# A two-layer encoder trunk on one core: another order of seven-product pairs in the FFN down projections, activation parts made three pairs ahead, and four row loads on another queue

## The chip, the cores and the metric

The kernel runs on one core of a Trainium2 chip. The metric is the device time of one execution in microseconds; lower is better. Several executions are timed, and the median is the number that counts. One further execution is profiled; its trace is what the views below are read from.

## The reference, cut to what matters

The input is 256 frames of 2048 values in float32. Two layers follow each other; each has a token mixer and a gated MLP with a causal convolution of width 3, and each of the four sub-layers ends in a layer norm of the scaled residual plus the sub-layer's output.

```python
def conv_ffn(x, w_up, conv_w, conv_b, w_down):
    h = x @ w_up                                   # 2048 -> 2 * 5504
    h = causal_depthwise_conv(h, conv_w) + conv_b  # width 3
    a, g = jnp.split(h, 2, axis=-1)
    return (jax.nn.silu(g) * a) @ w_down           # 5504 -> 2048

def reference(x, ...):
    for i in range(2):
        m = gmlp_mixer(x, ...) if i % 2 == 0 else mla_mixer(x, ...)
        x = layer_norm(ALPHA * x + m, ln_mix_g[i], ln_mix_b[i])
        f = conv_ffn(x, ...)
        x = layer_norm(ALPHA * x + f, ln_ffn_g[i], ln_ffn_b[i])
    return x
```

Layer 0 mixes by a spatial gating MLP (`gmlp_mixer`), layer 1 by latent attention (`mla_mixer`), whose first product makes a query latent and a key/value latent, each normalised before it is used.

## The kernel before, in words

All products keep float32 accuracy by splitting each operand into a high part (a cast to the fast float32 form) and a low part (the remainder). A product of two blocks is three matmuls: high by high, low by high, high by low. Weights come as chunks of 1 MB. The class `Feed` loads a chunk into a "raw" slot through SP's queue (`_load`, L93 and L98), makes the high part on ScalarE (wh, L127) and the low part on VectorE (wl, L130), both in "big" slots, and hands them to TensorE.

A down projection (`down`) multiplies 256 frames of activations by a weight of 5504 x 2048 (in the gMLP: 6144 x 2048). It runs in two halves of 1024 output columns; each half walks over the pairs of 128-row blocks of the weight in the order that `PLAN` writes out, the second half backwards. The frames form two blocks of 128, so that one pair and half a row of outputs is a 2 x 2 by 2 x 2 block product. There are three kinds of pair:

- "e", wide: eight products of 512 columns, 24 matmuls (`Banks.eight`).
- "s", seven: the Winograd form of Strassen's product with seven products, 21 matmuls (`Banks.seven`). VectorE first forms sums of the weight blocks (ts, L137), and those are split as well (th and tl beside wh and wl), so that five big tiles are needed, of which ts is free again once tl is made.
- "p", parked: the same seven products, but the four parts of the weights were made during the up projection before (`Feed.park`), stored to DRAM by POOL's queue, and are fetched again (`Feed.fetch`, L191) into "side" slots shortly before use. This takes neither ScalarE nor VectorE in the down projection.

The last pair, 21, is half a pair. With the plan of before a half has ten or nine pairs of kinds "s" and "p", 19 in both halves.

The activations have parts as well, made by `Acts.make`: high and low for a wide pair (two wide pairs share one slot, the room), and for a seven or parked pair also the sums (`turn`, L290 to L293) and their parts (L476, L477). In the trace dn04wx are the wide parts of pair 4 in layer 0, dn119sx the seven parts of pair 19 in layer 1, and wo4wx those of pair 4 in the gMLP's output projection. At each step `down` makes the parts of the pair at hand and of the pairs ahead, then calls `feed.next`, which splits the weights two pairs ahead and loads two more, and then issues the products. While the down projection runs, act0 to act5 hold the activations (four of them in big slots, two in side slots).

```python
SLOTS = {"big": 14, "raw": 3, "side": 6}
LEAD = 5
KEEP = {"wide": 4, "seven": 6, "parked": 6}
```

The order of work is written as a program; a scheduler at build time lets an instruction pass earlier ones of its engine when these would wait, and gives a tile a slot when one is free in that order. On each engine and each queue the resulting order is fixed: a DMA that waits for a slot holds up all that its queue issues later.

The residual comes back from DRAM in two halves. `ln.fetch` (L609, SP's queue) asks for a big slot when eight pairs of a half are left. After a half's last seven or parked pair, `rest` and `fold` (L443 to L447, L648) add up the shared sums, and `piece` (L654, L657) adds the accumulators.

A layer norm leaves its result without scale and shift; the residual needs these later. `Norm.restore` (L636 to L643) loads a piece of the two rows, spread to all partitions, into two tiles "lnp" of the tag "t2", and multiplies and adds on VectorE. It is called for norm 0 and norm 2 in the up projections and for norm 1 (`idx` 1) in the latent attention's kv product (mkv), four pieces of two rows each. After that product the latents are normalised (hqk, L937), and the key's rotary part is made (kr, L983).

Of the kernel before, what the change touches and what calls it, by code (L numbers as in the profile page):

```python
# [15 lines left out]
P = 128  # L16
# [7 lines left out]
NF_FF = DFF // P  # L24
# [33 lines left out]

PLAN = {NF_GM: ("0e 1e 2s 3e 4e 5s 6e 7e 8s 9e 10e 11s 12e 13e 14s 15e 16e 17s 18e 19e 20s 21e 22e 23e",
                "23e 22e 21e 20s 19e 18e 17s 16e 15e 14s 13e 12e 11s 10e 9e 8s 7e 6e 5s 4e 3e 2e 1e 0e"),  # L60
        NF_FF: ("0e 1p 2e 3s 4e 5p 6e 7s 8e 9p 10e 11s 12e 13p 14e 15s 16e 17p 18e 19s 20e 21e",
                "21e 20e 19s 18p 17e 16s 15e 14p 13s 12e 11e 10p 9s 8e 7e 6p 5s 4e 3e 2e 1e 0e")}
KINDS = {"e": "wide", "s": "seven", "p": "parked"}
LEAD = 5
KEEP = {"wide": 4, "seven": 6, "parked": 6}
# [2 lines left out]
def plan(n_k):  # L68

    return [[(int(t[:-1]), KINDS[t[-1]]) for t in line.split()] for line in PLAN[n_k]]  # L70
# [143 lines left out]
def trunk(ctx: ExitStack, tc: tile.TileContext, x, xT, gm_in, gm_wout, ffn_up, ffn_dn,  # L214
          ml_q, ml_kv, ml_b, ml_out, consts, w_sT, b_s, ropes, ln_rows, out):
    nc = tc.nc
# [10 lines left out]
    def slot(shape, name, dt=F32, tag="big"):  # L227
        return big.tile(shape, dt, tag=tag, name=name, bufs=SLOTS[tag])
# [76 lines left out]
    for j in range(4):  # L305
        t = slot([P, 4, S], f"xraw{j}", tag="side")
# [57 lines left out]
    def prod_b(acc, parts, hi, lo, pieces, first, last):  # L364

        xh, xl = parts
        for f, (o, w) in enumerate(pieces):
            mm(acc[f][:, :w], xh, hi[:, o : o + w], first, False)
            mm(acc[f][:, :w], xl, hi[:, o : o + w], False, False)
            mm(acc[f][:, :w], xh, lo[:, o : o + w], False, last)  # L370
# [114 lines left out]
    def down(n_k, src, tag, ln, acts, skew=SKEW):  # L485

        ln.begin()
        seq = plan(n_k)
        line = seq[0] + seq[1]
        late, at = [], 0  # L490
        fetched = max([i for i, t in enumerate(line) if t[1] == "parked"], default=len(line))
        for hf, units in enumerate(seq):
            n = len(units)
            last = [u for u, kind in units if kind != "wide"][-1]
            acc = Banks(f"{tag}{hf}", OWN + DIRECT if hf else DIRECT + OWN)
            for i, (u, kind) in enumerate(units):
                left = n - 1 - i if hf == 1 else n
                for n2, v2 in enumerate(line[at : at + 2]):
                    acts.make(*v2, "side" if at + n2 > fetched or at + n2 >= len(seq[0]) and v2[1] == "parked" else "big")
                if i == n - 8:  # L500
                    ln.fetch(hf)
                got = feed.next(splits=2 if left > 5 or left == 0 else 3, loads=2 if left > 2 or left == 0 else 1)
                if left == 6:
                    ln.prep()
                a, sums = acts.got[u]
                if left < skew:
                    late.append((a, *got))
                elif kind == "wide":
                    acc.eight(a, *got)
                else:  # L510
                    acc.seven(a, sums, *got, 512 if kind == "parked" else 0)
                    if u == last:
                        for j, t in enumerate(acc.rest()):
                            ln.fold(j // 2, 2 * hf + j % 2, t)
                at += 1
                for v2 in [v2 for v2 in acts.got if not any(v2 == w2 and n2 < KEEP[kind2]
                                                            for n2, (w2, kind2) in enumerate(line[at:]))]:
                    acts.got.pop(v2)
            if hf == 0:
                for j, m in enumerate(DIRECT):  # L520
                    ln.piece(j // 2, j % 2, acc.acc[m])

        def end(b, f):
            for i, (a, hi, lo) in enumerate(late):
                for j in range(len(a[b])):
                    prod_b([acc.acc[DIRECT[2 * b + f - 2]]], a[b][j], hi, lo, [(j * 1024 + (f - 2) * 512, 512)],
                           False, i == len(late) - 1 and j == len(a[b]) - 1)

        return [[None, None] + [acc.acc[DIRECT[2 * b + f]] for f in range(2)] for b in range(2)], end
# [60 lines left out]
    class Norm:  # L590
# [42 lines left out]
        def restore(self, f):  # L633

            row = []
            for j in range(2):  # L636
                t = tp.tile([P, 512], F32, tag="t2", name=f"lnp{self.idx}_{f}{j}", bufs=T2)
                src = ln_rows[2 * self.idx + j : 2 * self.idx + j + 1, f * 512 : (f + 1) * 512]
                nc.sync.dma_start(t, src.to_broadcast([P, 512]))
                row.append(t)  # L640
            for b in range(2):
                nc.vector.tensor_tensor(self.r(b, f), self.r(b, f), row[0], ALU.mult)
                nc.vector.tensor_tensor(self.r(b, f), self.r(b, f), row[1], ALU.add)  # L643
# [184 lines left out]

    ln = Norm(0, {})
    acc, end = down(NF_GM, pT, "wo", ln, acts)  # L830


# [12 lines left out]
    def ffn(layer, ln, acc, end, last):  # L845
# [28 lines left out]
        for gi in range(1, 22):  # L874
# [20 lines left out]
            if gi == 20:  # L895
                acts.make(*plan(NF_FF)[0][2])
        ln = Norm(2 * layer + 1, {}, old.put_away, last)
        return (ln, *down(NF_FF, act, f"dn{layer}", ln, acts, 4 if last else SKEW))

    ln, acc, end = ffn(0, ln, acc, end, False)  # L900
# [75 lines left out]
    for b in range(2):  # L976
# [3 lines left out]
        t = tp.tile([P, 4, ROPE], F32, tag="t1", name=f"kr2_{b}", bufs=T1)  # L980
# [291 lines left out]
```

## Time and profile before

| | us |
|---|---|
| median of 3 timed executions | 2493.83 |
| lowest and highest | 2492.6, 2495.56 |
| the profiled execution | 2495.52 |
| its span, first to last instruction | 2493.7 |

| stage (names in the trace) | from | to |
|---|---|---|
| gMLP products, output projection (v, u, wo) | 4.8 | 802.0 |
| layer 0: up projection (up) | 802.2 | 1284.9 |
| layer 0: down projection (dn0) | 1284.8 | 1511.5 |
| latent attention (mq to mo) | 1511.7 | 1775.3 |
| layer 1: up projection (up) | 1775.5 | 2258.2 |
| layer 1: down projection (dn1) | 2258.0 | 2483.1 |

The engines: PE is TensorE, DVE is VectorE, ACT is ScalarE, POOL is GpSimd, SP is SyncE. A row of waits names the instruction that waited, then what it waited for, then the total in us, the number of times and the longest. An engine's queue for DMAs has a "q" at its name (SPq). "issue" in a chain of waits is time in which the engine waited for nothing that the profile shows. A row of a group gives the count, then busy us and the mean ns of one instruction, then the idle time before them and what ended it. The ends of matmuls are modelled, so that a busy PE is not a PE at its peak; the number of matmuls in a window says more.

### The profile page before, as it was taken

The page shows a single profiled execution, that of the slowest core. Times are in us where ns is not written, and L with a number is a line of the kernel's source. Part 1 is how long each engine was busy: PE and PEld are TensorE (multiplying, and loading weights), DVE is VectorE, ACT ScalarE, POOL GpSimd, SP SyncE. Part 2 cuts the span into 40 slices and gives each one's busy share as a digit, 9 for nine tenths or more (in the row PEclk, how much of TensorE's full clock was granted, in tenths as well). Part 3 has the DMA queues.
Part 4 walks back from the last instruction along what each step waited for, and adds up shares of the span by engine and source line. Part 5 has one row for each costly group of instructions (what it writes and reads, how often), then busy time and mean ns, then how long its engine had stood idle before and what let it go on. Part 6 is the DMA issues. An engine that isn't in the chain of part 4 may idle for free. (4 is left out here: it accounts for less than half of the span.)

```text
span 2493.7 us, 33578 instructions
## 1 busy us (share of the span) xinstructions
PE 2471.9 (99%) x12989; PEld 2121.7 (85%) x12989; DVE 2009.0 (81%) x2822; ACT 1430.9 (57%) x1983; POOL 94.6 (4%) x183
## 2 busy tenths in 40 slices
PE   9999999999999999999999999999999999999998
PEld 7888888888888888888888788988888888888786
DVE  7999866679898788788687987856598878768797
ACT  6676544456555656566554556655566656555453
POOL 0000000000000000000001000000001000000010
PEclk9999999999999999999999999999999999999999
DMA  7556554556665689799568884544489798848885
GB/s 279 202 206 225 194 177 170 182 174 214 216 199 194 235 339 348 293 345 367 194 216 315 294 325 169 191 152 152 172 295 345 294 347 330 309 163 294 333 304 206
DMA packets 111809, 620.87 MB, mean 249 GB/s; under 512 B 10528, under 2 KB 11296, under 8 KB 63392
## 3 DMA queue, kind: packets, MB, share of 16 engines
q1 hardware_dynamic: 85440, 463.51, 52.0%
q0 software_dynamic: 26208, 155.20, 16.2%
q8 instruction: 102, 1.67, 0.2%
q14 instruction: 59, 0.48, 0.1%
HBM read 546.32 MB, written 72.35 MB: 248 GB/s over the span
## 5 line engine op out<-in xcount | busy, mean ns | idle before, releaser
L130 DVE TENSOR_TENSOR wl<-raw,wh 128x1024 fp32r<-128x1024 f32 (+4 forms) x691 | 965.1, 1418 | 221.9 <-ACT wh L127 132.7
L127 ACT CAST wh<-raw 128x1024 fp32r<-128x1024 f32 (+4 forms) x691 | 816.4, 1209 | 408.4 <-PE u L234 84.5
L234 PE MATMUL up<-xhl,wh 128*128 128x512 f32 x2624 | 611.9, 390 | 0.9 <-ACT wh L127 0.9
L234 PEld LDWEIGHTS up<-xhl,wh 128*128 128x128 f32 x2624 | 487.3, 188 | 99.4 <-ACT wh L127 1.8
L234 PEld LDWEIGHTS up<-xhl,wl 128*128 128x128 f32 x2624 | 325.8, 192 | 6.4
L234 PE MATMUL up<-xhl,wl 128*128 128x256 f32 x2624 | 328.1, 283 | 0.0
L234 PE MATMUL u<-xhl,wh 128*128 128x512 f32 x768 | 184.7, 393 | 0.1
L127 ACT CAST th<-ts 128x1536 fp32r<-128x1536 f32 x106 | 110.6, 1052 | 122.2 <-DVE ts L137 107.0
L234 PEld LDWEIGHTS u<-xhl,wh 128*128 128x128 f32 x768 | 141.1, 188 | 31.6 <-issue 3.8
L130 DVE TENSOR_TENSOR tl<-ts,th 128x1536 fp32r<-128x1536 f32 x106 | 125.4, 1219 | 2.2 <-PE v_p L234 1.5
L234 PEld LDWEIGHTS u<-xhl,wl 128*128 128x128 f32 x768 | 95.4, 192 | 2.0
L234 PE MATMUL u<-xhl,wl 128*128 128x256 f32 x768 | 96.0, 283 | 0.0
L234 PE MATMUL mo<-wh,oT 128*128 128x512 f32 x256 | 83.1, 404 | 0.3 <-DVE oT L1109 0.3
L137 DVE TENSOR_TENSOR ts<-ts,raw 128x512 f32<-128x512 f32 x106 | 72.9, 688 | 1.6
L234 PE MATMUL v_q<-wh,xhl 128*128 128x512 f32 x224 | 69.9, 393 | 1.0 <-ACT wh L127 1.0
L137 DVE TENSOR_TENSOR ts<-raw 128x1024 f32<-128x1024 f32 x53 | 64.6, 1220 | 0.2 <-PE v_q L234 0.2
L234 PE MATMUL v_p<-wh,xhl 128*128 128x512 f32 x192 | 59.7, 390 | 0.4 <-ACT wh L127 0.4
L234 PEld LDWEIGHTS mo<-wh,oT 128*128 128x128 f32 x256 | 45.4, 189 | 7.6 <-DVE oT L1109 0.6
L234 PEld LDWEIGHTS v_q<-wh,xhl 128*128 128x128 f32 x224 | 42.3, 189 | 10.3 <-ACT wh L127 1.7
L234 PE MATMUL mo<-wl,oT 128*128 128x512 f32 x128 | 50.2, 392 | 0.0
L154 DVE TENSOR_TENSOR praw<-praw 128x512 f32<-128x512 f32 x72 | 49.4, 686 | 0.5
L686 ACT ACTIVATE lny<-lnt,lncol 128x128 f32<-128x128 f32 x96 | 36.6, 472 | 15.6 <-PE lnt L682 15.6
(1844 smaller groups left out, 4186.6 us busy)
## 6 DMA issues: line engine op xcount, KB each, us to landing
raw<-in_ffn_up_dram SPq DMA_DIRECT2D x172, 1024.0 KB, 6.7
raw<-in_gm_in_dram SPq DMA_DIRECT2D x93, 1024.0 KB, 4.8
raw<-in_ffn_dn_dram SPq DMA_DIRECT2D x66, 1024.0 KB, 7.1
raw<-in_gm_wout_dram SPq DMA_DIRECT2D x48, 1024.0 KB, 5.2
praw<-in_ffn_dn_dram POOLq DMA_DIRECT2D x18, 1024.0 KB, 14.4
keptth<-pth POOLq DMA_DIRECT2D x18, 1024.0 KB, 6.3
kepttl<-ptl POOLq DMA_DIRECT2D x18, 1024.0 KB, 8.9
fth<-keptth POOLq DMA_DIRECT2D x18, 1024.0 KB, 9.5
```

The costliest lines, as they stand in the source:

```text
L127: cast = self.nc.scalar.copy(hi, raw)
L130: self.nc.vector.tensor_tensor(lo, raw, hi.bitcast(F32), ALU.subtract)
L137: add = lambda o, a, b: self.nc.vector.tensor_tensor(o, a, b, ALU.add)
L154: add = lambda o, a, b: pin(nc.vector.tensor_tensor(o, a, b, ALU.add))
L234: recent[0] = nc.tensor.matmul(o, l, r, start=start, stop=stop, skip_group_check=True)
L686: nc.scalar.activation(y[:, j], t[:, j * P : (j + 1) * P], AF.Identity, bias=lncol[:, o : o + 1], scale=lncol[:, g : g + 1])
```

## The change

The plan of the FFN down projections has another order of kinds. In the first half the parked pairs are 6, 11 and 15 instead of 5, 9, 13 and 17, beside pair 1; in the second half they are 19, 15, 11 and 7 instead of 18, 14, 10 and 6. The first half has nine pairs with seven products instead of ten, the second nine as before. In `down`, which the gMLP's output projection uses too, parts are made for three pairs (the one at hand and two more) instead of two. The rows for norm 1 are loaded by POOL's queue instead of SP's.

```diff
-        NF_FF: ("0e 1p 2e 3s 4e 5p 6e 7s 8e 9p 10e 11s 12e 13p 14e 15s 16e 17p 18e 19s 20e 21e",
-                "21e 20e 19s 18p 17e 16s 15e 14p 13s 12e 11e 10p 9s 8e 7e 6p 5s 4e 3e 2e 1e 0e")}
+        NF_FF: ("0e 1p 2e 3s 4e 5e 6p 7e 8s 9e 10e 11p 12e 13s 14e 15p 16e 17s 18e 19s 20e 21e",
+                "21e 20e 19p 18e 17s 16e 15p 14e 13s 12e 11p 10s 9e 8s 7p 6e 5s 4e 3e 2e 1e 0e")}
...
-                for n2, v2 in enumerate(line[at : at + 2]):
+                for n2, v2 in enumerate(line[at : at + 3]):
...
-                nc.sync.dma_start(t, src.to_broadcast([P, 512]))
+                (nc.gpsimd if self.idx == 1 else nc.sync).dma_start(t, src.to_broadcast([P, 512]))
```

## The prediction

> **What bounds the kernel now.** I read the page first, then the waits of TensorE over the whole run, then the two stages where they fall by windows, by the order of time and by the chain of waits.
>
> ```profile
> span 2493.7 us, 33578 instructions
> PE 2471.9 (99%) x12989; PEld 2121.7 (85%) x12989; DVE 2009.0 (81%) x2822; ACT 1430.9 (57%) x1983; POOL 94.6 (4%) x183
> ```
>
> TensorE is busy for 99% of the span, so a change can gain only TensorE's few waits, and every matmul it adds is paid in full. Those of PE's waits that bear on the change (us in total, times, longest):
>
> ```profile
> PE dn_q L234 <- ACT dn019sx L476: 1.5, 1, 1.5
> ...
> PE dn_q L234 <- ACT dn119sx L476: 1.1, 1, 1.1
> ...
> PE ct L945 <- DVE hqk L937: 0.9, 1, 0.9
> PE dn_e L234 <- DVE dn017wx L480: 0.7, 1, 0.7
> PE dn_e L234 <- DVE dn117wx L480: 0.7, 1, 0.7
> PE krt L990 <- ACT kr L983: 0.6, 1, 0.6
> PE wo_q L234 <- DVE wo4wx L480: 0.6, 1, 0.6
> PE dn_q L234 <- DVE dn120wx L480: 0.6, 1, 0.6
> ```
>
> Five of these stand in the FFN down projections (dn0 and dn1 are layers 0 and 1; dn019sx is the activation parts of pair 19, "s" for seven products, "w" wide, "p" parked). What they really cost shows when matmuls are counted. Six matmuls take 1.36 us, 0.227 each (first fence below). Then windows: length, PE busy and matmuls in it, other engines in the first two rows only, the granted clock, DMA share, GB/s.
>
> ```profile
> 2259.53 1.36 PE dn_p L234 x6
> ```
> ```profile
> 1324.00:1344.00 20.00, 20.00 (x90) 16.57 (x89) 16.23 (x22) 10.27 (x12) 2.11 (x4) 1.00 0.93 336
> ...
> 1404.00:1424.00 20.00, 19.32 (x86) 15.46 (x85) 19.52 (x29) 11.37 (x12) 2.11 (x4) 1.00 0.59 203
> ```
> ```profile
> 1381.00:1391.00 10.00, 8.28 (x29) 0.83 0.88 320
> 1411.00:1416.00 5.00, 4.32 (x20) 1.00 0.69 233
> 2353.00:2361.00 8.00, 6.64 (x28) 1.00 1.04 386
> 2366.00:2371.00 5.00, 4.42 (x20) 1.00 0.92 374
> 2383.00:2388.00 5.00, 4.35 (x20) 1.00 0.65 231
> ```
>
> An undisturbed 20 us shows 90 matmuls: 20 / 0.227 is 88, and two more reach over the edges. So 10, 8 and 5 us would show 46, 37 and 24. Missing are 17, 4, 9, 4 and 4: 3.9 and 0.9 us in layer 0, 2.0, 0.9 and 0.9 us in layer 1. The two down projections lose 8.6 us. The first loss is larger than its wait, because the matmuls after it come slowly:
>
> ```profile
> 1386.12 1.05 PE L234 MATMUL dn_p<-wh,dn019sx 128*128 128x512 f32 x2
> 1386.98 0.63 PE L234 MATMUL dn_p<-wl,dn019sx 128*128 128x512 f32 x1
> ```
>
> Two matmuls start within 0.86 us, 0.43 each, at the granted clock of 0.83 in that window. The Trainium skill ("TensorE: Matmul & The Clock Gate", Why this matters for your kernels) sets the danger line at idle gaps of about 3 us; the trace disagrees, since the wait here was 1.5 us plus a second of 0.2. By that rule the slow stretch would not come from the wait and would stay, and the sum below would be smaller by 3.9 - 1.7 = 2.2 us.
>
> Why the parts of pair 19 are late is told by the chain of waits (start, length, what), layer 1:
>
> ```profile
> 2325.56 2.28 DVE tl L130 x2
> ...
> 2328.76 15.28 DMA raw<-in_ffn_dn_dram
> ...
> 2355.94 0.62 ACT dn119sx L476
> ```
> ```profile
> SPq L609 <- DVE tl L130: 30.0, 2, 15.0
> ```
>
> This is a shortage of "big" slots. The residual's fetch (L609) has to find one, and stands 15.0 us at the head of SP's queue until pair 15's tl frees its ts slot. The weights of pairs 18 and 19 queue behind it; then the fetch, weight loads and parked pair 17 travel together, and a load takes 15.28 us. ACT's cast waits for it, pair 19's sums follow, and dn119sx comes last: its room is asked for after pair 19's five weight tiles. Counted from the code, act0 to act3 hold 4 slots, the residual 1, two parts' rooms 2, pair 18's weights 2 and pair 19's 5: that is 14 of 14.
>
> **The change, part by part.**
>
> *Plan.* One parked pair less in each FFN. A wide pair makes 24 matmuls, a seven or parked one 21: 3 x 0.227 = 0.68 us more per FFN, +1.36 us, all on PE. The up projection loses per FFN one parking job (load, casts, sums, four stores), and the down projection four fetches; these lie beside TensorE's work in stages where none of the rows above stands, so I cost them at nothing. The pair that becomes wide needs one load, one cast and one subtraction. The durations (count, busy, mean ns):
>
> ```profile
> L130 DVE TENSOR_TENSOR wl<-raw,wh 128x2048 fp32r<-128x2048 f32 x15 | 34.4, 2290 | 15.1 <-ACT wh L127 10.3 <-issue 4.8
> L130 DVE TENSOR_TENSOR tl<-ts,th 128x1536 fp32r<-128x1536 f32 x8 | 14.0, 1752 | 0.0
> L130 DVE TENSOR_TENSOR wl<-raw,wh 128x1536 fp32r<-128x1536 f32 x8 | 14.0, 1751 | 0.0
> L137 DVE TENSOR_TENSOR ts<-ts,raw 128x512 f32<-128x512 f32 x17 | 11.7, 686 | 0.2
> L137 DVE TENSOR_TENSOR ts<-raw 128x1024 f32<-128x1024 f32 x9 | 11.0, 1218 | 0.0
> L130 DVE TENSOR_TENSOR tl<-ts,th 128x512 fp32r<-128x512 f32 x8 | 5.5, 684 | 0.0
> ```
> ```profile
> L127 ACT CAST wh<-raw 128x2048 fp32r<-128x2048 f32 x15 | 28.7, 1911 | 10.6 <-DMA raw<-in_ffn_dn_dram 9.6 <-PE dn_p L234 1.0
> ```
>
> A seven costs DVE 1.22 + 2 x 0.69 + 1.75 + 1.75 + 0.68 = 6.8 us, a wide pair 2.29, a parked one nothing. ACT 1.91 and DVE 2.29 for the new wide pair fall into the first half, where the row of 1324 shows DVE 16.2 and ACT 10.3 of 20: covered. If that cover were gone, each would cost up to 4.2 us per FFN.
>
> The order matters more than the number. In the first half the fetch for parked 15 now starts when 11 ends, about a pair before the residual's and not with it, and pair 17's weights are loaded ahead of the residual on SP. By the code's order the residual can take one of the three slots (two weights, one room) that wide pair 12 gives up when it ends; I expect the 15 us block to shrink to a few us and the late load to go. In the second half pair 19 is parked and its parts are kept from the first half, so DVE loses 6.8 us of work just where it runs 19.5 of 20 (row of 1404) and where PE waits for dn017wx and dn120wx. Against that, sevens now stand at 17 and 19 with one wide pair between, and at 10 and 8: in the first half act0 to act3, residual and three rooms leave 6 slots for weights, and 17s (4 once ts is free) and 18e (2) fill them. So 18e's two slots come only when 16e ends: cast 1.91 + subtraction 2.29 = 4.2 us, in the 7 x 3 x 0.227 = 4.77 us of 17s. That holds with 0.5 us to spare; 19s then gets its slots from 17s with 5.44 us of 18e as cover, its 6.8 us of DVE ending about when tl is wanted, three products (2.04 us) into the pair.
>
> *Parts three pairs ahead.* No instruction is added; the casts and subtractions of parts go ahead of one more pair's weights on ACT and DVE. Queued behind them are that pair's casts, with a pair or more of slack, and one room is held a pair longer. This takes dn019sx and dn119sx out from behind pair 19's sums, and wo4wx out of the gMLP's output projection: -0.6 us, the row's wait (bounds 0 and -0.6).
>
> What stays of the 8.6 us: at best nothing; at worst all, for the shortage itself stays. Nearest rows: one loss of 0.9 us per FFN, like dn017wx, since DVE stays near full at the change of halves, and 0.55 us at 18e or 20e with so little to spare. I take 2 x 1.45 = 2.9, near the lower end, because the two rows that carry most of the loss hang on the block at L609. So -5.7.
>
> *Residual rows by POOL's queue* (layer 1's mixer only). SP's queue and who waits there:
>
> ```profile
> 1542.29 2.29 SPq L639 DMA_DIRECT2D lnp<-in_ln_rows_dram  x5
> ```
> ```profile
> ACT wh L127 <- DMA raw<-in_ml_b_dram: 12.5, 3, 5.7
> DVE res L643 <- DMA lnp<-in_ln_rows_dram: 1.3, 1, 1.3
> POOL praw L164 <- PE sc L234: 193.7, 1, 193.7
> ```
>
> The first row leaves at 1542.29, behind the raw loads of the kv weights. DVE waits 1.3 us for a row, which delays the subtractions that free raw slots, so the ml_b loads, ACT's cast and, behind the cast, the squares that hqk and kr hang on: PE loses 0.9 + 0.6 there. On POOL the eight issues pass those loads; POOL is idle for 193.7 us around, and only two small memsets for the rotary keys and the next parking load stand behind. Bounds: -1.5 (both waits) to +1.3 (the rows come later by as much as DVE waits now). I take -1.2, for 1.3 us of lead is most of 1.5. The Trainium skill ("DMA: Bandwidth & Descriptors", Issuing engines are not separate DMA queues) says that transfers from all queues share the same engines and that another issuer saves issue time only; by that rule this term would be 0 and the sum -4.9.
>
> Sum: +1.36 - 5.7 - 0.6 - 1.2 = -6.1 us. The profiled execution took 2495.52 us, 1.8 beyond its span; 2489.4 for it, and 2487.7 on the median of 2493.83.
>
> **Rivals.** *The shortage only moves.* Each FFN keeps its 4.3 us, now at 18e's weights instead of 19's parts: +1.36 - 0.6 - 1.2 = -0.4, 2493.4. For it: the slots are 14 before and after, and the plan asks for more. Against: the late residual made the trouble, and it moves off.
>
> *The rows gain nothing*: their 1.2 us stay, because ml_b's loads share the transfers with the rows as before and ACT waits 12.5 us for them, not for rows: 2488.9. This is where the Trainium skill's rule on issuing engines leads.
>
> *The slow stretch is not the wait's* and stays: 2.2 us less, 2489.9. For it: it follows only one of the five losses. Against: it begins right behind the longest wait, in the one window with a clock under 1. The Trainium skill's rule on idle gaps leads here.
>
> *Slower: two sevens round one wide pair.* If the wide pair's two slots come only when the seven ahead has ended, PE stands for the 4.2 us of cast and subtraction and then runs some eight matmuls at 0.43 instead of 0.23: 5.8 us, at 18e. At 9e, with more slots free as act tiles end, only the subtraction may be late, 2.3. Together 8.1 per FFN, 16.2: 16.2 - 8.6 + 1.36 - 1.8 = +7.2, 2501.0. It decides from 7 us of waits per FFN on. For it: 6 slots for 6 tiles. Against: 16e's slots come 4.77 us earlier than that.
>
> **How the numbers follow.** 0.2% is 5 us, about what a measurement of this kernel can tell from no change. Forecast 0.55, by itself 2484 to 2489. Rows gain nothing 0.07, slow stretch stays 0.03 and shortage moves 0.12, all within 5 us: 0.22. Slower 0.23. The range goes from 2483.5 (all of 8.6, 0.6 and 1.5 gone: -9.3 from the median, and 1 less) to 2501.0, the slower case's price; left out are some 0.04 below and half of 0.23 above.
>
> **What would show it.** Right: no wait of PE for dn019sx, dn119sx or the w parts of 17 to 20; SP's wait at L609 for tl well under 30 us; 978 instead of 975 matmuls in each down projection; hqk and kr gone from PE's waits; no window of the down stages with a clock under 1. Wrong: PE waiting for wh or wl of dn_q at 18, 19, 9 or 8, or for a parked tile; the shortage has then moved, and its length decides between the rivals.

## The result and the profile after

| | before | after |
|---|---|---|
| median of the timed runs, same chip | 2493.45 us (2492.51 to 2495.56) | 2486.59 us (2485.0 to 2487.36, 6 runs) |
| ratio to before, 95% interval | 1 | 0.997 [0.9957, 0.9983] |
| profiled execution, time and span | 2495.52, 2493.7 us | 2486.63, 2484.8 us |

The changed kernel is faster by 0.3%, 6.9 us on the medians. A second series further below gave 0.9977 [0.9967, 0.9987]. The forecast was 2487.7.

The page of the changed kernel (the span, then busy time, share and instructions of each engine):

```profile
span 2484.8 us, 33520 instructions
PE 2468.0 (99%) x12995; PEld 2122.3 (85%) x12995; DVE 1992.9 (80%) x2802; ACT 1424.6 (57%) x1979; POOL 89.0 (4%) x173
```

PE has 12995 matmuls where it had 12989: six more, three for each FFN down projection, 978 instead of 975. VectorE's work fell by 16.1 us. All waits of PE that the view names, and SP's waits at the residual's fetch (us in total, times, longest):

```profile
PE wo_q L234 <- DVE h_u L393: 1.7, 1, 1.7
PE warm L234 <- POOL idle L280: 1.3, 1, 1.3
PE v_q L234 <- ACT wh L127: 1.2, 1, 1.2
PE up L234 <- ACT wh L127: 0.9, 2, 0.5
PE up L234 <- DVE wl L130: 0.5, 1, 0.5
```
```profile
SPq L609 <- PE dn_q L234: 19.6, 2, 9.8
SPq L609 <- DVE tl L130: 16.2, 2, 8.1
```

No wait of a down projection is left, and none for hqk, kr or wo4wx. SP still stands at L609, but in the first half for 9.8 us and not for 15.0; the 8.1 us for a tl belong to the second half. The windows over the places of the losses (length, PE, PEld, DVE, ACT, POOL busy with counts, granted clock, DMA share, GB/s):

```profile
1364.00:1384.00 20.00, 20.00 (x90) 16.57 (x89) 14.23 (x17) 9.93 (x11) 2.12 (x4) 1.00 0.77 278
1384.00:1404.00 20.00, 20.00 (x90) 16.55 (x89) 20.00 (x25) 8.60 (x9) 0.53 (x1) 1.00 0.74 265
1404.00:1424.00 20.00, 20.00 (x90) 16.57 (x89) 18.06 (x31) 10.70 (x12) 2.11 (x4) 1.00 0.95 352
...
2360.00:2380.00 20.00, 20.00 (x90) 16.57 (x89) 20.00 (x28) 8.98 (x8) 1.59 (x3) 1.00 0.81 297
```

Each 20 us holds 90 matmuls, the count of an undisturbed window, at a clock of 1.00, even where DVE is busy for all 20. For comparison, the kernel before in the first two:

```profile
1364.00:1384.00 20.00, 18.51 (x82) 14.92 (x80) 12.55 (x17) 7.63 (x8) 2.11 (x4) 1.00 1.03 400
1384.00:1404.00 20.00, 19.77 (x80) 15.99 (x80) 18.81 (x25) 8.87 (x9) 0.00 (x0) 0.91 0.78 283
```

Where the time came from is read by stage, from the first matmul of a stage to the first of the next, in the profiles (worked out from the traces, us; "again" is a second build and profile of the same program; "mkv" reaches from the first mkv matmul to the first of the products that use the normalised latents, "u" is the gMLP's gated half up to its output projection wo; the down projection of layer 1 is counted to the start of its own last matmul):

| stage | before | before again | after | after again | three ahead | plan |
|---|---|---|---|---|---|---|
| u | 291.38 | 291.48 | 293.19 | 291.40 | 291.34 | 291.51 |
| wo | 254.26 | 254.27 | 253.26 | 253.26 | 253.27 | 254.25 |
| dn, layer 0 | 226.94 | 226.88 | 222.53 | 222.53 | 223.09 | 223.42 |
| mkv | 46.03 | 43.90 | 43.85 | 43.85 | 43.87 | 43.87 |
| mo | 116.86 | 116.88 | 116.50 | 116.53 | 116.50 | 116.50 |
| up, layer 1 | 482.48 | 482.44 | 483.40 | 486.72 | 482.40 | 482.42 |
| dn, layer 1 | 224.74 | 224.66 | 221.45 | 221.45 | 221.97 | 222.29 |
| span | 2493.75 | 2490.74 | 2484.79 | 2486.61 | 2482.90 | 2484.52 |

The down projections give 4.4 + 3.3 = 7.7 us and wo gives 1.0. These repeat to 0.1 us. The 2.1 us of mkv do not: the same program without the change has 43.90 in its second profile. Against the gain stand 1.8 us in u, in one of two profiles, and 0.9 to 4.3 us in layer 1's up projection.

### The profile page after: what moved, and what is told of

It reads as the page before. It is cut to its first block, busy times and chain, and to the rows that moved or that the text cites. A ratio compares the mean times of both kernels' runs of the same rounds, so it can differ in the third digit from the quotient of the medians.

```text
span 2484.8 us, 33520 instructions
## 1 busy us (share of the span) xinstructions
PE 2468.0 (99%) x12995; PEld 2122.3 (85%) x12995; DVE 1992.9 (80%) x2802; ACT 1424.6 (57%) x1979; POOL 89.0 (4%) x173
## 5 line engine op out<-in xcount | busy, mean ns | idle before, releaser
L686 ACT ACTIVATE lny<-lnt,lncol 128x128 f32<-128x128 f32 x96 | 36.6, 471 | 15.6 <-PE lnt L682 15.5
L171 DVE TENSOR_TENSOR pwl<-praw,pwh 128x1536 fp32r<-128x1536 f32 x16 | 28.1, 1755 | 20.4 <-ACT pwh L170 20.4
```

The costliest lines, as they stand in the source:

```text
L171: pin(nc.vector.tensor_tensor(lo[:, 0:cols], raw[:, o : o + cols], hi[:, 0:cols].bitcast(F32), ALU.subtract))
L686: nc.scalar.activation(y[:, j], t[:, j * P : (j + 1) * P], AF.Identity, bias=lncol[:, o : o + 1], scale=lncol[:, g : g + 1])
```

## The experiments

Theory: SP's queue is blocked at L609 until a slot comes free; what then travels together is too much, pair 19's load comes late, and its sums hold dn019sx. Whatever breaks this chain heals most. The rivals were that the slots themselves are too few, that only the plan or only the look-ahead heals, and that the rows carry a part.

**The plan alone** (`plan_only`):

```diff
-        NF_FF: ("0e 1p 2e 3s 4e 5p 6e 7s 8e 9p 10e 11s 12e 13p 14e 15s 16e 17p 18e 19s 20e 21e",
-                "21e 20e 19s 18p 17e 16s 15e 14p 13s 12e 11e 10p 9s 8e 7e 6p 5s 4e 3e 2e 1e 0e")}
+        NF_FF: ("0e 1p 2e 3s 4e 5e 6p 7e 8s 9e 10e 11p 12e 13s 14e 15p 16e 17s 18e 19s 20e 21e",
+                "21e 20e 19p 18e 17s 16e 15p 14e 13s 12e 11p 10s 9e 8s 7p 6e 5s 4e 3e 2e 1e 0e")}
```

> The kernel before with the new order of pairs alone. Theory A (the plan moves the residual's fetch off pair 15's tl, and pair 19 parked in the second half unloads VectorE): the down projections lose under 1.5 us each instead of 4.8 and 3.9 us, no wait for dn017wx or dn120wx; the waits for wo4wx (0.6), hqk (0.9) and kr (0.6) stay; with +1.36 for the two seven-product pairs less, about -5 us. Rival B (only making the parts earlier counts): PE still waits for dn019sx and dn119sx, and as sevens stand at 17 and 19 it waits 2 us or more in each layer; 0 to +3 us in all.

Measured: 2487.4 us against 2493.89, ratio 0.9973 [0.9962, 0.9983]. Waits of the plan alone:

```profile
PE wo_q L234 <- DVE wo4wx L480: 0.6, 1, 0.6
PE dn_q L234 <- DVE dn05sx L477: 0.2, 1, 0.2
PE dn_q L234 <- DVE dn15sx L477: 0.2, 1, 0.2
...
SPq L609 <- PE dn_q L234: 29.4, 4, 11.0
```

The five waits of the down projections are gone and two of 0.2 us have come at pair 5; wo4wx stays. The plan alone heals most of the loss in the down projections: with 223.42 and 222.29 us they stay 0.9 and 0.8 us above the changed kernel's, which has the same matmuls.

**Three pairs ahead alone** (`ahead_only`):

```diff
-                for n2, v2 in enumerate(line[at : at + 2]):
+                for n2, v2 in enumerate(line[at : at + 3]):
```

> The kernel before with parts for three pairs instead of two, nothing else. Theory A: dn019sx and dn119sx no longer come last, so 3.9 + 2.0 us of losses shrink, but the residual's fetch still stands for 15 us and the slots are still 14 of 14, so PE waits for weights of pair 19 instead: 1 to 2 us stay per layer; dn017wx, dn117wx and dn120wx (0.9 us each) stay; the start of the gMLP's output projection gets the new 1.7 us wait of the changed kernel and loses the 0.6 of wo4wx: about -2 us. Rival B: all five losses of the down projections go, about -8 us there.

Measured: 2485.15 us, ratio 0.9967 [0.9954, 0.9979]. Theory A missed, and what came is near Rival B: the gain is 8.7 us, of which the two down projections give 3.9 and 2.8. The wait at wo's start that Theory A counted with did not come.

```profile
PE dn_q L234 <- DVE dn018px L477: 0.9, 1, 0.9
PE dn_q L234 <- DVE dn118px L477: 0.9, 1, 0.9
...
SPq L609 <- PE dn_p L234: 14.6, 2, 7.3
```

Under the old plan the five waits are gone too; one new one of 0.9 us, at parked 18, stands in each FFN. The tl has vanished from L609's releasers: in the first half SP now waits 7.3 us for a product of PE. But the residual does not leave earlier by that: it goes at 1354.72 us, where the kernel before had 1354.62. SP only comes to stand there later, with one more weight load already issued. The larger change is in the order on ACT and DVE (start, length, what; pair 19's parts in layer 0, first before, then in this run with its residual and its pair 19's tl):

```profile
1383.02 0.61 ACT L476 CAST dn019sx<-dn019st 128x512 fp32r<-128x512 f32 x1
```
```profile
1369.48 0.62 ACT L476 CAST dn019sx<-dn019st 128x512 fp32r<-128x512 f32 x1 [2.11 <-DVE dn019st L290]
...
1375.20 2.36 DVE L130 TENSOR_TENSOR tl<-ts,th 128x1536 fp32r<-128x1536 f32 x2 [0.18 <-PE dn_p L234]
...
1354.72 0.82 SPq L609 DMA_DIRECT2D res<-resd  x2
```

Before, the parts were cast right behind pair 19's tl, which ended at 1382.46. Here they come 13.5 us earlier and ahead of that tl, so that the weights no longer hold them. The slots are the same 14, held longer. So plan and look-ahead break one chain at two links, and their effects do not add: the plan heals 7.3 us of the loss in the down projections (they are 6.0 us shorter, and its added matmuls hide 1.4), the look-ahead 6.6, and the whole change 9.1.

**The rows alone** (`rows_only`):

```diff
-                nc.sync.dma_start(t, src.to_broadcast([P, 512]))
+                (nc.gpsimd if self.idx == 1 else nc.sync).dma_start(t, src.to_broadcast([P, 512]))
```

> The kernel before with norm 1's rows on POOL's queue alone. Theory A: the waits for hqk and kr go, 1.5 to 2.5 us less between the first mq and the first upf of layer 1, everything else as before: -1.5 to -2.5 us. Rival (another issuer saves issue time only): the two waits stay, 0 us; then the changed kernel's 2.5 us in this stage came out of the down projection's end.

Measured: 2493.12 us, ratio 0.9997 [0.9988, 1.0007]: no gain clear of noise. The interval reaches from 3.0 us less to 1.7 us more, so it does not exclude the 1.2 us of the prediction either. In this run's profile hqk and kr are indeed gone from PE's waits, and mkv takes 43.83 us; whether the edit did that is what the second profile of the program before has to tell.

**The residual by POOL's queue** (`res_pool`), plan and look-ahead as before:

```diff
-                nc.sync.dma_start(t[:, b, :], src)
+                (nc.sync if self.away is None else nc.gpsimd).dma_start(t[:, b, :], src)
```

> The kernel before with the residual's fetch (norms 1 and 3) on POOL's queue instead of SP's; slots, plan and parts as before. Theory A (SP's queue stands 15 us behind the fetch, and so the weights of 18 and 19 come late): the loads of 18 to 20 leave some 8 us earlier, the cast of 18 no longer waits for a load, and the losses at pair 19 (3.9 and 2.0 us) fall under 1 us each; dn017wx stays: -4 to -5 us. Rival C (the slots alone: the room of dn019sx is asked for after pair 19's five tiles, whenever the loads come): the wait for dn019sx stays at 1 us or more, and the time within 1.5 us of before.

Measured: 2488.89 us, ratio 0.998 [0.9971, 0.999], 5.0 us less.

```profile
PE dn_q L234 <- DVE wl L130: 1.6, 1, 1.6
...
PE dn_e L234 <- DVE dn017wx L480: 0.9, 1, 0.9
PE dn_e L234 <- DVE dn117wx L480: 0.8, 1, 0.8
```

And POOL's queue at the residual:

```profile
1357.26 1.09 POOL L609 DMA_DIRECT2D res<-resd  x2
```

The number of slots and the order in which `down` asks for parts and weights were not changed, only the queue that issues the residual. Both waits for pair 19's parts are gone, although the residual leaves later than before (1357.26 us for 1354.62), right behind the fetches of parked 17 and without a wait of its own. So what hurt was not that the residual came late but what SP's queue held up behind it; the block at its head is thereby shown as the cause of these waits. The waits of the change of halves (017wx, 117wx) stay, and at 1405 us the low part of pair 19's weights is late once, in the second half. The two down projections take 225.22 and 222.39 us, 4 us less than before.

**The program before, once more** (`before_again`), because the rows alone had gained nothing:

> The kernel before once more, unchanged, for a second profile. In the profiles of four variants, also those that leave norm 1's rows on SP's queue, the stretch from the first mkv to the first qn takes 43.8 to 43.9 us, against 46.0 before. Theory X (the 2.1 us belong to that one execution, whose ml_b loads took 9.0 us instead of some 7.2): 43.9 us here, and no waits for hqk and kr. Theory Y (they belong to the order of the program before): 46.0 us again, with waits of 0.9 and 0.6. The five waits of the down projections return in both.

Measured: 2492.5 us in one run, span 2490.7. The kernel before shows hqk and kr among PE's waits in its first profile and not in this one. What ACT waited for the ml_b loads, first profile and second:

```profile
ACT wh L127 <- DMA raw<-in_ml_b_dram: 12.5, 3, 5.7
```
```profile
ACT wh L127 <- DMA raw<-in_ml_b_dram: 9.8, 3, 5.7
```

The two waits on which the rows' term was built, 0.9 and 0.6 us, are not in every execution of the program. They are not wholly an accident either: `ahead_again`, further below, has 0.3 us at kr and 44.48 us in mkv, also with the rows on SP's queue, while the five profiles with the rows on POOL's queue all have 43.8 to 43.9. Two late profiles of nine against none of five are too few to say whether POOL's queue spares them.

**The second half's order alone** (`second_half`):

```diff
-                "21e 20e 19s 18p 17e 16s 15e 14p 13s 12e 11e 10p 9s 8e 7e 6p 5s 4e 3e 2e 1e 0e")}
+                "21e 20e 19p 18e 17s 16e 15p 14e 13s 12e 11p 10s 9e 8s 7p 6e 5s 4e 3e 2e 1e 0e")}
```

> The kernel before with the second half of the new plan alone (19 pairs with seven products, 19 parked in the second half). Theory A (a seven less for VectorE behind the change of halves): the waits for dn017wx, dn117wx and dn120wx go (0.9 us each), dn019sx and dn119sx stay with 3.9 and 2.0 us within 1 us; the two down projections lose about 6 us instead of 8.6. Rival (a fetch for 19 right behind that of 17 fills the queues): waits for fwh or wh of 0.5 us or more come in their place.

Measured: 2492.04 us in one run, span 2490.2.

```profile
PE dn_q L234 <- ACT dn019sx L476: 1.5, 1, 1.5
...
PE dn_q L234 <- ACT dn119sx L476: 1.3, 1, 1.3
...
PE dn_q L234 <- DVE dn120wx L480: 0.6, 1, 0.6
...
PE dn_q L234 <- DVE dn14wx L480: 0.4, 1, 0.4
...
SPq L609 <- DVE tl L130: 30.0, 2, 15.0
```

Pair 19's waits and the 15.0 us stay, dn017wx and dn117wx are gone, as Theory A said. Against it, dn120wx keeps its 0.6 us in layer 1, and a wait of 0.4 us at pair 4 is new there. The down projections take 226.01 and 224.51 us, 0.9 and 0.2 less than before: the second half's order heals the waits for pair 17 and nothing else.

**The first half's order alone** (`first_half`):

```diff
-        NF_FF: ("0e 1p 2e 3s 4e 5p 6e 7s 8e 9p 10e 11s 12e 13p 14e 15s 16e 17p 18e 19s 20e 21e",
+        NF_FF: ("0e 1p 2e 3s 4e 5e 6p 7e 8s 9e 10e 11p 12e 13s 14e 15p 16e 17s 18e 19s 20e 21e",
```

> The first half's order of the new plan alone (parked 6, 11 and 15, sevens 3, 8, 13, 17 and 19), the second half's order as before. Theory (the order of fetches in the first half is what heals pair 19): SP's wait at L609 for tl is gone, PE's waits for dn019sx and dn119sx are gone (1.7 and 1.1 us before), no stretch of slow matmuls follows, dn017wx and dn117wx (0.7 each) stay because they are made at the change of halves under the old second half; both down projections about 2.5 to 3.5 us (layer 0) and 0.7 to 1.7 us (layer 1) shorter than before. Rival (pair 19 needs the second half's order or the longer look-ahead as well): dn019sx 1 us or more and the wait at L609 for tl at 10 us or more remain.

Measured: 2491.7 us in one run, span 2489.9.

```profile
PE dn_e L234 <- DVE dn021wx L480: 1.8, 1, 1.8
PE dn_e L234 <- DVE dn121wx L480: 1.8, 1, 1.8
...
SPq L609 <- PE dn_q L234: 22.0, 2, 11.0
SPq L609 <- PE dn_p L234: 20.2, 2, 10.1
```

The tl and pair 19's waits are gone, as the theory said. The wait at the change of halves falls on 21's parts and not on 17's, and is 1.8 us, not 0.7; so the two stages, which also carry the 0.7 us of added matmuls, are only 1.4 and 0.6 us shorter than before, less than expected (225.54 and 224.17 us, 3.0 and 2.7 above the changed kernel). The first half's order heals pair 19, the second half's pair 17; neither is enough alone.

**The old first half with the rest of the change** (`mixed19`): only the second line of the plan is new, parts go three pairs ahead, rows by POOL.

```diff
         NF_FF: ("0e 1p 2e 3s 4e 5p 6e 7s 8e 9p 10e 11s 12e 13p 14e 15s 16e 17p 18e 19s 20e 21e",
-                "21e 20e 19s 18p 17e 16s 15e 14p 13s 12e 11e 10p 9s 8e 7e 6p 5s 4e 3e 2e 1e 0e")}
+                "21e 20e 19p 18e 17s 16e 15p 14e 13s 12e 11p 10s 9e 8s 7p 6e 5s 4e 3e 2e 1e 0e")}
...
-                for n2, v2 in enumerate(line[at : at + 2]):
+                for n2, v2 in enumerate(line[at : at + 3]):
...
-                nc.sync.dma_start(t, src.to_broadcast([P, 512]))
+                (nc.gpsimd if self.idx == 1 else nc.sync).dma_start(t, src.to_broadcast([P, 512]))
```

> The changed kernel with the first half of the old plan (so 19 pairs with seven products in each FFN), the new second half, three pairs ahead, rows on POOL's queue. Theory A (three pairs ahead heals dn019sx, pair 19 parked heals the second half, and the pair given up buys nothing): no wait in the down projections, 0.68 us per layer less than the changed kernel in each; 2484 to 2485.5 us, unless the gap of 1.7 us at the start of the gMLP's output projection goes too (then 2483). Rival (the pair given up is what makes room): 1 us or more of waits per layer at pairs 17 to 19, 2487 us or more.

Measured: 2486.16 us, ratio 0.9964 [0.9951, 0.9976] against 2494.59: as good as the changed kernel. Layer 0's down projection is the shortest of all at 221.85 us and has no wait. Layer 1's, 222.43, has two waits at its end that layer 0's has not, against Theory A, and a wait at wo's start is there as in the changed kernel (u takes 292.64 us):

```profile
PE wo_q L234 <- DVE h_u L393: 1.2, 1, 1.2
PE dn_q L234 <- DVE dn12wx L480: 1.0, 2, 0.7
```

The two layers run the same order; which of them keeps its slack differs. The pair given up is thus not needed for the gain.

**The changed kernel with wo two pairs ahead** (`wo_two`):

```diff
-                for n2, v2 in enumerate(line[at : at + 3]):
+                for n2, v2 in enumerate(line[at : at + (3 if n_k == NF_FF else 2)]):
```

> The changed kernel with two pairs ahead again in the gMLP's output projection alone. Theory A (three pairs ahead there costs the new 1.7 us gap before its first matmul and gains the 0.8 us at wo4wx): gap gone, wo4wx's 0.8 us back, 1.0 us less: 2485.6 us. Rival (the gap comes from the plan by way of the build's order, whatever is made ahead): the gap stays and wo4wx returns, 2487.3 us.

Measured: 2487.22 us, ratio 0.9971 [0.996, 0.9982]. The stage u takes 291.36 us and the wait at wo's start is gone, wo4wx's 0.6 us is back (wo 254.24), and layer 1's up projection takes 485.33 us with four waits:

```profile
PE up L234 <- DVE wl L130: 1.8, 4, 0.6
...
PE wo_q L234 <- DVE wo4wx L480: 0.6, 1, 0.6
```

So the longer look-ahead in wo is what gives wo its 1.0 us. The stages are those of Theory A; that the time is the rival's 2487.3 comes from the up projection, which neither had in its sum. Whether the longer look-ahead also made the wait at wo's start can't be read from this one profile.

**The changed kernel once more** (`after_again`):

> The changed kernel once more, to tell what of its first profile belongs to the program. There PE stood 1.7 us at the start of the gMLP's output projection (for h_u of the last spatial stage's output) and 0.6 us more in layer 1's up projection; in both places one load had landed late (7.1 us for wout where other profiles have 5.3; 17.1 us for a parked tile). Theory (these are accidents of one execution's transfers): the stage before wo takes about 291.4 us again and up1 about 482.5, the span is 2482 to 2483. Rival (the plan or the longer look-ahead makes them): 293.2 and 483.4 again, span about 2484.8. Under both theories both down projections stand without a wait, 222.5 and 221.5 us.

Measured: 2488.25 us (2484.49 to 2491.04, 8 runs) against 2493.28, ratio 0.9977 [0.9967, 0.9987]. For u the theory holds: 291.40 us, no wait at wo's start. The load of wout that was issued at 532.6 us in the first profile and at 532.9 in this took, first and second:

```profile
raw<-in_gm_wout_dram SPq DMA_DIRECT2D x1, 1024.0 KB, 7.1
```
```profile
raw<-in_gm_wout_dram SPq DMA_DIRECT2D x1, 1024.0 KB, 5.3
```

The same program, 1.8 us apart, as much as the wait of 1.7. In `mixed19`, with its wait of 1.2 us, this load took 6.6; in the twelve other profiles it took 5.3 to 5.5, and there is no such wait. So a late load goes with the wait. Both late loads are among the five profiles with three pairs ahead in wo, none among the nine with two; whether that is chance stays open. For the up projection the theory fails: 486.72 us, with this wait and this window:

```profile
PE up L234 <- DVE wl L130: 1.8, 1, 1.8
```
```profile
1990.00:1994.00 4.00, 4.00 (x18) 3.76 (x19) 4.00 (x4) 3.48 (x3) 0.53 (x1) 0.57 0.26 66
```

The wait is 1.8 us, the matmuls after it come slowly at a mean granted clock of 0.57, and the stage is 4.3 us longer than undisturbed.

**Three pairs ahead, on one chip with the changed kernel** (`ahead_again`, the edit of `ahead_only`):

> The plan of before (19 sevens) with parts made three pairs ahead, and nothing else of the change, on one chip with the changed kernel. It spares the changed kernel's three matmuls per FFN (2 x 0.68 = 1.36 us) and had two waits for parts of parked 18 (2 x 1.08 = 2.16 us lost, dn0 and dn1 0.5 us longer each than in the changed kernel). Theory: with the accidents of transfers out, the sum over u, wo, the up and the down projections is 0.5 to 1.1 us above the changed kernel's, so the two times agree within 0.1%. Rival (its first time was no accident, the plan costs more than it gives once parts go three ahead): 1.5 us or more below the changed kernel on the same chip, ratio 0.9995 or less.

Measured: 2485.59 us (2485.05 to 2488.75, 6 runs), ratio to before 0.9967 [0.9955, 0.9979]; against the changed kernel's 2488.25 that is 2.7 us less (0.9989). In the down projections it is behind by 0.5 and 0.6 us, as the theory said, but it has 482.47 us in layer 1's up projection, where the changed kernel has 486.72. The rival's number came. In the profiles the difference lies in the up projection and not in the products saved; but the plan may be what makes that stage longer (next run), so the rival's cause, that the plan costs more than it gives, is not ruled out. All runs taken together, the median is 2485.4 us (12 runs) for this one line and 2487.3 (14) for the whole change. The one line alone is at least as good as the whole, with six matmuls fewer; the two intervals to before overlap, so "better" rests on the medians only.

**The plan alone once more** (`plan_again`), for the up projection:

> The plan alone once more, for layer 1's up projection. All three profiles with the plan, three pairs ahead and the rows on POOL's queue lose time there (482.45 us undisturbed; 483.4 to 486.7 with it), and so does the new first half alone (483.7); the third parking load, issued near 1918 us, took 16.4 to 18.5 us in those four and 14.2 in the first profile of the plan alone, which lost nothing. Theory (the plan's eight parking jobs leave the third one's load at an unlucky place, and its first profile was the exception): the load takes over 16 us and the stage 483.2 us or more. Rival (the plan alone does not do it): under 15.6 us and 482.6 us or less. The down projections stay 223.4 and 222.3 us under both.

Measured: 2487.14 us in one run. The third parking load took 17.3 us, as the theory wanted, and the stage 482.57, as the rival wanted: neither holds as a whole. The five profiles of layer 1's up projection in which that load took 16.3 us or more:

| kernel | third parking load, us | stage, us |
|---|---|---|
| after | 17.2 | 483.40 |
| after again | 18.5 | 486.72 |
| wo two pairs ahead | 17.5 | 485.33 |
| first half's order | 16.4 | 483.69 |
| plan again | 17.3 | 482.57 |

In the nine other profiles of the experiments and of before it took 13.2 to 15.5 us, and the stage 482.4 to 482.6. All five have the plan's new first half, with eight parking jobs for nine: of the six profiles with it five have the late load, of the eight without it none. So the lateness is very probably the plan's, though how the plan brings it about stays open. A late third parking load goes with every loss, but does not always bring one.

## Why the prediction was right, point by point

*The bound.* Right. PE was busy for 99% of the span, and the gain is what its waits cost, less the added matmuls.

*The plan's matmuls, +1.36.* Right: 12995 for 12989. The three products more in each FFN also show in `mixed19` (19 sevens, no wait, 221.85) against the changed kernel (222.53): 0.68 us, the term's own size.

*What of the 8.6 us stays: 2.9 predicted, 0 measured.* This is the term that was mis-sized. The two stages went down by 4.41 and 3.29 us; with 1.36 added back, 9.1 us healed, all of the loss that the windows had counted (8.6) and half a microsecond more. The row I leaned on, 0.9 at the change of halves because DVE stays near full, was no reason: the rows of 1384 and, over layer 1's change of halves, of 2360 show DVE at 20.00 of 20 and PE without a gap. DVE's fullness alone holds nobody. The second allowance, 0.55 at 18e or 20e, has no wait in the changed kernel either.

*The block at L609.* The mechanism is shown by `res_pool`: SP issued nothing from 1339.55 to 1354.62 us, and with that block gone pair 19's waits are gone. That the plan's first half heals the same waits is shown by `first_half`. The size was off: "a few us" was 9.8 us, and 11.0 with the plan alone. What changed is not so much the block as what waits behind it. Of the DMA issues from 1350 to 1358 us (KB each, median us to landing), before:

```profile
raw<-in_ffn_dn_dram SPq DMA_DIRECT2D x2, 1024.0 KB, 16.5
res<-resd SPq DMA_DIRECT2D x2, 512.0 KB, 10.3
```

and after:

```profile
res<-resd SPq DMA_DIRECT2D x2, 512.0 KB, 6.8
raw<-in_ffn_dn_dram SPq DMA_DIRECT2D x1, 1024.0 KB, 7.9
```

Before, two weight loads go out together with the residual, among the four fetches of parked 17, and need 16.5 us. After, one goes with it and needs 7.9.

*Three pairs ahead.* wo4wx: -0.6 predicted, and the stage gave 1.0; `wo_two` takes it back. The prediction had this edit take dn019sx and dn119sx out from behind pair 19's sums, and the trace of `ahead_only` shows that mechanism: the cast at 1369.48 us instead of 1383.02, ahead of the tl. That the edit does this alone, without the plan, and also heals the waits at the change of halves, was foreseen neither there nor in Theory A of the experiment. SP also had one load more out before it stood at L609; how much of the cure that is was not tried by itself.

*The rows, -1.2: not found.* The term took the waits of one profile for waits of the program. The 2.1 us in mkv stand in one profile of before and are missing in the next of the same program, and the rows alone gave 0.9997 [0.9988, 1.0007], which can't tell -1.2 us from nothing. The rival that gave the rows nothing fits best. The rule beside it, that transfers from all queues share the same engines and another issuer saves only issue time (the Trainium skill, "DMA: Bandwidth & Descriptors", Issuing engines are not separate DMA queues), is not contradicted by that number. It says nothing against `res_pool`, where another queue did gain 5.0 us: there SP's queue stood still for a slot for 15.0 us.

*The slow stretch.* Right: with the wait gone the down projections show no granted clock under 1. All four profiles with the 1.5 to 1.6 us wait at dn019sx (before, before again, the rows alone, the second half alone) have the stretch behind it, and none of the ten others has it there. The rival that it would stay falls.

*The slower case.* Two sevens round one wide pair cost nothing: no wait at 18e, 9e, 17s or 8s in either layer. The 0.5 us of slack that was worked out for 18e was about right: in layer 0 the cast of its weights starts at 1372.67 us, when 17s starts, the subtraction ends at 1376.90, and 18e's first matmul starts at 1377.5.

*The sum.* -6.1 predicted for the profiled execution; 2495.52 - 2486.63 = 8.9 measured there, 6.9 on the medians, 5.0 in the later series. The first profile of before holds 2.1 us in mkv that its second has not; from second profile to second profile the spans differ by 4.1 us (2490.74 to 2486.61), of which the down projections give 7.6 and wo 1.0, and layer 1's up projection takes back 4.3. So it is in part luck that the forecast of 2487.7 lies within 1.1 us of the measured median; it was near by terms that cancel: 3.4 us too little from the down projections and 0.4 from wo, against 1.2 too much from the rows and the 0.9 to 4.3 us in layer 1's up projection, where the prediction costed the plan at nothing because none of its rows stood in that stage. That reason was no good: a stage without a wait before can have one after.

## What to carry to other kernels

When a DMA that waits for a slot stands at the head of a queue, look at what stands behind it: here the damage was the weight loads that it held up. Another queue, another order, or work put ahead of those weights each broke the chain, and the gains did not add, so try such edits singly before they are added up. A wait that is seen in one profile is a term of a sum only if a second profile of the same program shows it; here 2.1 us in mkv and 1.8 us in u stood in one of two profiles of the same program. And an engine that is full for 20 us is not by itself a reason for a wait.

## What the runs showed of the hardware

The slow stretch after a wait has one length in these runs and no plain threshold. Its records show 3.41 us at a granted clock of 0.50 in each of the five profiles that have one: the four named above, and the changed kernel again in its up projection. The first of them, in the kernel before:

```profile
1385.15:1388.56 3.41, 3.41 (x10) 2.66 (x9) 3.09 (x3) 2.64 (x5) 0.00 (x0) 0.50 0.72 282
```

A clock of 0.83, 0.72 or 0.57 in a longer window is the mean of this stretch and full clock around it. Windows with the wait in them or right behind it; first the program before again (layer 0, then layer 1), then the first half's order:

```profile
1383.00:1389.00 6.00, 5.78 (x17) 4.33 (x18) 5.48 (x6) 5.01 (x6) 0.00 (x0) 0.72 0.78 274
...
2354.00:2360.00 6.00, 5.78 (x26) 4.68 (x26) 5.48 (x7) 4.67 (x6) 0.00 (x0) 1.00 0.95 328
```
```profile
1409.00:1412.00 3.00, 1.21 (x5) 0.68 (x5) 3.00 (x4) 1.18 (x2) 0.00 (x0) 1.00 0.56 175
1412.00:1415.00 3.00, 3.00 (x14) 2.44 (x13) 3.00 (x5) 1.40 (x2) 0.00 (x0) 1.00 0.88 310
```

A wait of 1.5 us with one of 0.2 behind it is followed by a mean clock of 0.72 (17 matmuls in 6 us), one of 1.1 with 0.2 is not (26), and the longer one of 1.8 us at dn021wx is not either (14 in 3 us, the full rate). The 1.8 us in layer 1's up projection was followed by 0.57. Inside the stages such a stretch comes only behind a wait of 1.5 us or more in all of these runs, and not behind each of them; what decides whether it comes is open. The Trainium skill ("TensorE: Matmul & The Clock Gate", Why this matters for your kernels) puts the danger line at idle gaps of about 3 us; here the clock fell behind 1.5 + 0.2 us.
